# Three rings for FFN weight tiles, Down's raw weights issued five steps ahead, sums moved behind the lows, and first-visit banks copied by ScalarE

## The chip, the cores and the metric

The program runs on one core of one Trainium2 chip. The metric is the device time of one execution in microseconds (us). Engines: PE is TensorE (matmuls), DVE is VectorE, ACT is ScalarE, POOL is GpSimd, SP is SyncE (it only issues DMAs here).

## The reference

One inference step of a decoder layer for 512 prompt rows and 32 sample rows (544 columns in the kernel): stick-breaking attention and gated DeltaNet on one projection, cross attention, then SwiGLU. The change is in the last part, where D_MODEL is 2048 and FFN_HIDDEN is 5632, all in fp32:

```python
x = x + concat([o_sb, o_gdn]) @ p['w_out']
...
x = x + xo @ p['w_xo']
hf = rmsnorm(x, p['norm_ffn_g'])
gate, up = jnp.split(hf @ p['w_gate_up'], 2, axis=-1)
x = x + (jax.nn.silu(gate) * up) @ p['w_down']
```

## The kernel before

**Numbers.** An fp32 product is made of three matmuls in a reduced type (fp32r): hi·hi, hi·lo, lo·hi. For a weight tile, ScalarE casts the high part (`wh`) and VectorE subtracts it from the tile, which gives the low part (`wl`). Both FFN products use a scheme of 7 block products in place of 8 (products q = 1 to 7), so that four of the products take sums and differences of weight blocks; VectorE makes these (`sum`).

**Order.** `Work` is a table written out by hand: `at(tick, place, do)`. Ticks run upward, within a tick the places run upward, and each engine gets its instructions in that order. No engine waits for a tick: an engine goes on with the next instruction as soon as what it needs is there. So the table sets what is queued behind what on each engine.

**Gate/up** (class `GateUp`, 44 columns j, 7 ticks each): `load` issues four raw weight blocks of 512 KB on SP ("21", "11", "22", "12"), `sum` makes four differences (L1711), `high` (L1718) and `low` (L1722) split each of the seven left operands, `matmuls` (L1729) does 24 matmuls of 128x272 per tick. The hidden activations `u` are cast to `hs` and stored to DRAM (`hT`, by SP), to be fetched later by POOL's queue as `pr` operands of Down.

**Down** begins at tick `t_down` = 308 and has 88 steps (class `Step`) of 42 matmuls (L1783), one step a tick, for pairs of output columns m and groups g of hidden rows. A step loads its raw weights with two DMAs of 256 KB (L1750, tile `raw`), makes three sums (`sums`, L1760 to L1762), two highs (`high`, L1767: 0 of the raw weights, 1 of the sums) and two lows (`low`, L1773). It accumulates in four PSUM banks, P16 (128x544), P7 (128x272), P45 and P23 (128x544). Step p's loads stand at tick p − 4, its sums at p − 2, its highs and lows at p − 1.

A block of output columns is visited several times, and between visits the banks are kept in SBUF (tiles `a`). `take` does that: on the first visit VectorE copies P16 and P7 (L1833) and ScalarE P45 and P23 (L1831); on a middle visit VectorE adds P16 and P7 to what was kept (L1835), while P45 and P23 are read back and seeded: ScalarE's `before` (L1811) copies the kept part into the bank ahead of the next visit of that block. On the last visit `combine` joins the banks (ScalarE's s1, L1843; VectorE's L1844, L1846, L1848, L1849, L1851), and `out` transposes the results on TensorE into one PSUM tile (`aux`, L967), scales them on ScalarE (`y`, L2046) and stores them. The three parts of `out` stand at places 32.5 and 35.5 of the next tick and 32.5 of the one after. Steps 0 to 7 are the first visits of the eight blocks (group 0), 8 to 11 are group 1 of one half, 12 to 19 take groups 1 and 2 by turns, 20 to 71 the groups up to 8 in the same way, and 72 to 87 are the last visits, two steps each (groups 9 and 10). On first and last visits the products stand in the order 1, 6, 7, 4, 5, 2, 3, on middle visits 4, 5, 2, 3, 1, 6, 7, so that there P16's bank is touched only after 24 of the 42 matmuls.

**Tiles.** All weight tiles have one size (128x1024 fp32). `Ffn.tile` takes `wl` and raw "12" from a ring of 4 (`vp`) and everything else (raw, sums, `wh`) from one ring of 9 (`wp`). A tile of a ring waits for the last reader of the one that had the slot before. `fetch` (L1954) gets the `pr` operands of a group, 14 tiles of 272 KB, spread over ticks.

Of the kernel before, what the change touches and what calls it, by code (L numbers as in the profile page):

```python
# [8 lines left out]
F32 = mybir.dt.float32  # L9
F32R = mybir.dt.float32r  # L10
# [5 lines left out]
P = 128  # L16
# [24 lines left out]
W_TILES = 13  # L41
# [1606 lines left out]
class GateUp:  # L1648
# [3 lines left out]
    def __init__(self, f, j):  # L1652
# [5 lines left out]
        for x, tick in (("21", -8), ("11", -8), ("22", -7), ("12", -3)):  # L1658
            at(self.t0 + tick, 5, lambda x=x: self.load(x))
# [41 lines left out]
    def load(self, x):  # L1701
        f, c0 = self.f, self.cols[x[0] == "2"]
        self.a[x] = f.tile(F32, "raw", x == "12")
# [3 lines left out]
    def sum(self, q):  # L1707

        x, y = {5: ("21", "22"), 7: ("21", "11"), 6: ("22", 7), 3: ("12", 6)}[q]
        self.a[q] = self.f.tile(F32, "sum")  # L1710
# [5 lines left out]
    def high(self, q):  # L1716
        self.hi[q] = self.f.tile(F32R, "wh")
        self.f.c.nc.scalar.copy(self.hi[q], self.left(q))  # L1718

    def low(self, q):  # L1720
        self.lo[q] = self.f.tile(F32R, "wl", True)
# [17 lines left out]
class Step:  # L1739
# [5 lines left out]
    def load(self):  # L1745
        raw = self.f.tile(F32, "raw")
# [9 lines left out]
    def sums(self):  # L1756

        a, v = self.raw, self.c.nc.vector
        self.sum = b = self.f.tile(F32, "sum").rearrange("p (s m) -> p s m", s=4)
# [4 lines left out]
    def high(self, i):  # L1764
        x = (self.raw[:, 1:], self.sum)[i]
        hi = self.f.tile(F32R, "wh").rearrange("p (s m) -> p s m", s=4)[:, : 3 + i]
# [3 lines left out]
    def low(self, i):  # L1770
        x = (self.raw[:, 1:], self.sum)[i]
        lo = self.f.tile(F32R, "wl", True).rearrange("p (s m) -> p s m", s=4)[:, : 3 + i]
# [16 lines left out]
class Down:  # L1789
# [35 lines left out]
    def take(self, bank):  # L1825
# [4 lines left out]
        elif bank in (P45, P23):  # L1830
            self.c.nc.scalar.copy(x, self.c.bank[bank])  # L1831
        elif new:
            self.c.nc.vector.tensor_copy(x, self.c.bank[bank])  # L1833
# [20 lines left out]
class Ffn:  # L1854
# [29 lines left out]
    def tile(self, dt, name, own=False):  # L1884

        return (self.c.vp if own else self.c.wp).tile([P, 8 * P], dt, tag="w", name=name, bufs=4 if own else W_TILES - 4)

# [73 lines left out]
    def down(self):  # L1961
# [11 lines left out]
        tiles = [(pair, n, k) for n in (3, 1, 2, 0) for pair in range(2) for k in range(2 if n else 1)]  # L1973
        for g in range(11):
            a, b = used[g - 3][1] + 1 if g > 2 else (0, 0, 5)[g], used[g][0] - 1
            for i, x in enumerate(tiles):
                tick = t0 + a + i * (b - a) // 14 if g else t0 - (6 if i < 6 else 4)
# [4 lines left out]
    def step(self, p, s, nb):  # L1982

        at, tick, b = self.work.at, self.t_down + p, s.block
        seed = lambda block, *banks: [block.before(x) for x in banks if block]

        early = lambda n: tick - n if p >= n else self.t_down - 2 * (n - p)
        at(early(4) if p >= 4 else self.t_down - 12 + 2 * p, 95, s.load)

        place = lambda n, x, y: (early(n), x if early(n) >= self.t_down else y)  # L1990
        at(*place(2, 25, 62), s.sums)
        for i in range(2):
            at(early(1), 20 + i, lambda i=i: s.high(i))
# [243 lines left out]
```

## Time and profile before

| | us |
|---|---|
| median of 3 runs (lowest to highest) | 2971.8 (2969.07 to 2971.97) |
| the profiled execution | 2973.26 |
| its span in the profile | 2971.3 |
| mean granted clock of TensorE | 0.991 of full speed |

Gate/up runs from about 1530 to 2457 of the span, Down from 2457 to 2964. The profile shows when each engine worked, what each instruction waited for, and the chain of work that ended last. Idle time counts where TensorE is held up, since it is the engine with the most work.

### The profile page before, as it was taken

How to read it: one execution, taken by the hardware profiler on the slowest of the kernel's cores; microseconds unless marked ns; L12 is line 12 of the kernel's file. 1: busy time of each engine (PE TensorE's matmuls, PEld its weight loads, DVE VectorE, ACT ScalarE, POOL GpSimd, SP SyncE). 2: the span in 40 equal slices, each digit the busy share in tenths (PEclk: the TensorE clock that was granted, in tenths of full speed). 3: DMA queues.
4: the chain of work that ended last, by engine and by line, in shares of the span. 5: the costliest groups of instructions: out<-in, count | busy, mean ns of one | idle time of the engine just before them, and what ended most of it. 6: DMA issues, size and time to landing. Idle time of an engine off the chain costs nothing.

```text
span 2971.3 us, 56668 instructions
## 1 busy us (share of the span) xinstructions
PE 2868.1 (97%) x22122; PEld 2769.5 (93%) x22122; DVE 2079.2 (70%) x3334; ACT 1485.9 (50%) x2812; POOL 673.1 (23%) x916
## 2 busy tenths in 40 slices
PE   8999999999999999999979999999999999999999
PEld 7999999889899989998769999999999998999999
DVE  5776775655656665446488788878787777777786
ACT  5545443444555564334564444444444445445666
POOL 3211212312112100003222333333323234110110
PEclk9999999999999999999989999999999999999999
DMA  7323233454553684533444555555554558666653
GB/s 218 91 76 91 78 88 94 131 156 125 156 151 108 187 262 143 151 98 90 161 123 134 163 169 163 157 156 165 165 153 149 159 174 249 199 200 181 197 161 110
DMA packets 640420, 444.37 MB, mean 150 GB/s; under 512 B 36411, under 2 KB 566664, under 8 KB 640152
## 3 DMA queue, kind: packets, MB, share of 16 engines
q1 hardware_dynamic: 608328, 386.31, 44.3%
q0 software_dynamic: 22176, 42.90, 4.7%
q10 hardware_dynamic: 9648, 11.54, 1.1%
q8 instruction: 174, 2.85, 0.4%
q14 instruction: 94, 0.77, 0.1%
HBM read 360.07 MB, written 80.58 MB: 148 GB/s over the span
## 4 chain that ended last, share of the span: by engine, by line
PE 55%; DMA 4%; DVE 3%; ACT 1%; issue 1%; SPq 0%; ACTq 0%; DVEq 0%
PE gu L1729 31%; PE bank L1783 11%; PE mm L215 7%; DMA raw<-in_w_down 3%; PE aux L1349 2%; PE mm L1537 2%; DVE wl L1773 1%; PE aux L967 1%; PE aux L757 0%; DMA wr<-in_w_xo 0%; DVE sum L1760 0%; DVE sum L1761 0%; PE aux L706 0%; DVE wl L204 0%; DMA mem<-in_mem_prompt 0%
## 5 line engine op out<-in xcount | busy, mean ns | idle before, releaser
L1729 PE MATMUL gu<-pr,wh 128*128 128x272 f32 x4928 | 673.0, 289 | 6.8 <-ACT pr L1604 5.6
L1729 PEld LDWEIGHTS gu<-pr,wh 128*128 128x128 f32 x4928 | 640.4, 189 | 9.3 <-ACT pr L1604 6.8
L215 PE MATMUL mm<-ah,wh 128*128 128x272 f32 (+1 forms) x2464 | 537.6, 298 | 5.1 <-ACT ah L328 4.0
L215 PE MATMUL mm<-al,wh 128*128 128x272 f32 (+1 forms) x2464 | 523.4, 291 | 0.7 <-DVE al L246 0.7
L215 PE MATMUL mm<-ah,wl 128*128 128x272 f32 (+1 forms) x2464 | 514.9, 289 | 0.1
L1783 PE MATMUL bank<-pr,wh 128*128 128x272 f32 x2464 | 473.4, 291 | 8.5 <-DVE a L1833 4.5
L215 PEld LDWEIGHTS mm<-ah,wh 128*128 128x128 f32 (+1 forms) x2464 | 391.1, 188 | 28.3 <-issue 8.5
L1783 PEld LDWEIGHTS bank<-pr,wh 128*128 128x128 f32 x2464 | 391.2, 191 | 10.5 <-ACT bank L1811 4.8
L204 DVE TENSOR_TENSOR wl<-wr,wh 128x512 fp32r<-128x512 f32 (+1 forms) x366 | 262.0, 720 | 193.9 <-ACT wh L203 183.9
L215 PEld LDWEIGHTS mm<-al,wh 128*128 128x128 f32 (+1 forms) x2464 | 388.6, 188 | 5.4 <-issue 2.0
L203 ACT CAST wh<-wr 128x512 fp32r<-128x512 f32 (+1 forms) x366 | 224.4, 616 | 332.1 <-PE mm L215 272.4
L215 PEld LDWEIGHTS mm<-ah,wl 128*128 128x128 f32 (+1 forms) x2464 | 385.6, 188 | 2.5 <-DVE wl L204 0.5
L1783 PE MATMUL bank<-pr,wl 128*128 128x272 f32 x1232 | 359.2, 292 | 13.6 <-DVE wl L1773 12.6
L1729 PE MATMUL gu<-pr,wl 128*128 128x272 f32 x2464 | 359.7, 288 | 1.3 <-DVE wl L1722 1.3
L1729 PEld LDWEIGHTS gu<-pr,wl 128*128 128x128 f32 x2464 | 328.3, 189 | 1.6 <-DVE wl L1722 1.6
L1718 ACT CAST wh<-sum 128x1024 fp32r<-128x1024 f32 x176 | 185.0, 1051 | 175.5 <-DVE wl L1722 162.6
L1722 DVE TENSOR_TENSOR wl<-sum,wh 128x1024 fp32r<-128x1024 f32 x176 | 228.6, 1299 | 33.9 <-ACT wh L1718 30.3
L1783 PEld LDWEIGHTS bank<-pr,wl 128*128 128x128 f32 x1232 | 235.2, 191 | 17.7 <-DVE wl L1773 17.7
L1718 ACT CAST wh<-raw 128x1024 fp32r<-128x1024 f32 x132 | 139.0, 1053 | 107.6 <-DVE sum L1711 83.9
L1722 DVE TENSOR_TENSOR wl<-raw,wh 128x1024 fp32r<-128x1024 f32 x132 | 189.5, 1435 | 0.1
L1711 DVE TENSOR_TENSOR sum<-raw,sum 128x1024 f32<-128x1024 f32 x88 | 115.8, 1316 | 99.8 <-PE gu L1729 99.8
L1954 POOL DMA_DIRECT2D pr<-hT x154 | 81.8, 548 | 272.9 <-PE bank L1783 247.9
(530 smaller groups left out, 4331.4 us busy)
## 6 DMA issues: line engine op xcount, KB each, us to landing
raw<-in_w_gate_up SPq DMA_DIRECT2D x176, 512.0 KB
wr<-in_w_in SPq DMA_DIRECT2D x108, 512.0 KB
raw<-in_w_down SPq DMA_DIRECT2D x176, 256.0 KB
hT<-hs SPq DMA_DIRECT2D x154, 272.0 KB
pr<-hT POOLq DMA_DIRECT2D x154, 272.0 KB, 6.6
page<-in_cache_sb_k SPq DMA_DIRECT2D x128, 128.0 KB
page<-in_cache_sb_v SPq DMA_DIRECT2D x64, 256.0 KB
wr<-in_w_out SPq DMA_DIRECT2D x32, 512.0 KB
```

Source lines behind the costliest of these rows:

```text
L203: nc.scalar.copy(hi[:, :m, :n], raw[:, k : k + m, :n])
L204: nc.vector.tensor_sub(lo[:, :m, :n], raw[:, k : k + m, :n], hi[:, :m, :n].bitcast(F32))
L215: c.nc.tensor.matmul(ps[:n, h, :HT], l[:, :n], r[:, h * HT : (h + 1) * HT], start=first and i == 0, stop=last and i == 2,)
L967: c.nc.tensor.transpose(ps[:, a * P : (a + 1) * P], src[:, a * P : (a + 1) * P], c.ident)
L1349: nc.tensor.matmul(ps[:, :256], l, r, start=k == 0 and n == 0, stop=k == 7 and n == 2)
L1537: nc.tensor.matmul(ps[:, 0, :HT], l, r[:, cols], start=k == 0 and i == 0, stop=k == 3 and i == 2)
L1711: self.f.c.nc.vector.tensor_sub(self.a[q], self.a[x], self.a[y])
L1718: self.f.c.nc.scalar.copy(self.hi[q], self.left(q))
L1722: self.f.c.nc.vector.tensor_sub(self.lo[q], self.left(q), self.hi[q].bitcast(F32))
L1729: self.f.c.nc.tensor.matmul(bank, w[:, i * P : (i + 1) * P], self.f.pairs[i].op[q][r], start=q in (1, 5) and n == 0, stop=n == 23, skip_gr ...
L1783: self.c.nc.tensor.matmul(self.c.bank[bank][:, o], t[x][:, s, i * P : (i + 1) * P], pairs[i].op[q][r], start=new and not (i or n), stop=se ...
L1954: self.c.nc.gpsimd.dma_start(t, self.hT[2 * g + pair, :, max(0, 2 * n - 1) + k])
```

## The change

Tiles come from three rings: `vp` of 4 for `wl` and raw "12" as before; `wa` of 4 for all `wh` and gate/up's sums 5 and 3; `wp` of 5 for gate/up's raws "21", "11", "22" and sums 7 and 6, and for Down's raws and sums by turns. So in Down raw p takes the slot of the sum of step p − 4, and the sum of step p the slot of raw p − 1. Gate/up's raw "22" is loaded at tick −5 in place of −7.

Down's raws are loaded at tick p − 5 (steps 0 and 1 at −8, step 2 at −5, 3 at −4, 4 at −1). The sums of step k + 2 stand at place 52 of tick k, behind the lows of k + 1 (places 31 and 50) and ahead of the takes (60, 61), where they stood at 25, ahead of both lows. First visits copy all four banks on ScalarE, in the order P16, P7, P45, P23. Group 2's fetches start at tick 7 after `t_down` (they started at 5), group 3's at 13 (8); the others as before. Lines below the first lie 1 lower in the new file (L1760 becomes L1759), and from `take` on 3 lower.

```diff
...
-W_TILES = 13
...
@@ -1655,7 +1654,7 @@
         self.cols = k * P, HID + k * P
         self.a, self.hi, self.lo = {}, {}, {}
         at = f.work.at
-        for x, tick in (("21", -8), ("11", -8), ("22", -7), ("12", -3)):
+        for x, tick in (("21", -8), ("11", -8), ("22", -5), ("12", -3)):
             at(self.t0 + tick, 5, lambda x=x: self.load(x))
         for q, tick in ((7, -4), (5, -3), (6, -2), (3, 1)):
             at(self.t0 + tick, 50, lambda q=q: self.sum(q))
@@ -1700,25 +1699,25 @@
 
     def load(self, x):
         f, c0 = self.f, self.cols[x[0] == "2"]
-        self.a[x] = f.tile(F32, "raw", x == "12")
+        self.a[x] = f.tile(F32, "raw", f.c.vp) if x == "12" else f.tile(F32, "raw", f.c.wp, 5)
         w = f.c.w_gu.rearrange("(i t p) m -> t p i m", t=2, p=P)[x[1] == "2"]
         f.c.nc.sync.dma_start(self.a[x].rearrange("p (i m) -> p i m", m=P), w[:, :, c0 : c0 + P])
 
     def sum(self, q):
 
         x, y = {5: ("21", "22"), 7: ("21", "11"), 6: ("22", 7), 3: ("12", 6)}[q]
-        self.a[q] = self.f.tile(F32, "sum")
+        self.a[q] = self.f.tile(F32, "sum", self.f.c.wp, 5) if q in (7, 6) else self.f.tile(F32, "sum", self.f.c.wa)
         self.f.c.nc.vector.tensor_sub(self.a[q], self.a[x], self.a[y])
 
     def left(self, q):
         return self.a[{1: "11", 2: "12", 4: "22"}.get(q, q)]
 
     def high(self, q):
-        self.hi[q] = self.f.tile(F32R, "wh")
+        self.hi[q] = self.f.tile(F32R, "wh", self.f.c.wa)
         self.f.c.nc.scalar.copy(self.hi[q], self.left(q))
 
     def low(self, q):
-        self.lo[q] = self.f.tile(F32R, "wl", True)
+        self.lo[q] = self.f.tile(F32R, "wl", self.f.c.vp)
         self.f.c.nc.vector.tensor_sub(self.lo[q], self.left(q), self.hi[q].bitcast(F32))
 
     def matmuls(self, q):
@@ -1743,7 +1742,7 @@
         self.f, self.c, self.block, self.visit, self.g, self.first, self.last = f, f.c, block, visit, g, first, last
 
     def load(self):
-        raw = self.f.tile(F32, "raw")
+        raw = self.f.tile(F32, "raw", self.c.wp, 5)
         self.raw = raw.rearrange("p (s t i m) -> p s t (i m)", s=2, t=2, i=2)
 
         for s, m in ((1, self.block.m), (0, self.block.m + 1)):
@@ -1756,20 +1755,20 @@
     def sums(self):
 
         a, v = self.raw, self.c.nc.vector
-        self.sum = b = self.f.tile(F32, "sum").rearrange("p (s m) -> p s m", s=4)
+        self.sum = b = self.f.tile(F32, "sum", self.c.wp, 5).rearrange("p (s m) -> p s m", s=4)
         v.tensor_sub(b.rearrange("p (x s) m -> p x s m", s=2)[:, :, 0], bc(a[:, 0:1], [P, 2, 2 * P]), a[:, 1:3])
         v.tensor_sub(b[:, 1], a[:, 1], b[:, 2])
         v.tensor_sub(b[:, 3], a[:, 3], b[:, 1])
 
     def high(self, i):
         x = (self.raw[:, 1:], self.sum)[i]
-        hi = self.f.tile(F32R, "wh").rearrange("p (s m) -> p s m", s=4)[:, : 3 + i]
+        hi = self.f.tile(F32R, "wh", self.c.wa).rearrange("p (s m) -> p s m", s=4)[:, : 3 + i]
         self.c.nc.scalar.copy(hi, x)
         self.hi = (self.hi + [hi]) if i else [hi]
 
     def low(self, i):
         x = (self.raw[:, 1:], self.sum)[i]
-        lo = self.f.tile(F32R, "wl", True).rearrange("p (s m) -> p s m", s=4)[:, : 3 + i]
+        lo = self.f.tile(F32R, "wl", self.c.vp).rearrange("p (s m) -> p s m", s=4)[:, : 3 + i]
         self.c.nc.vector.tensor_sub(lo, x, self.hi[i].bitcast(F32))
         self.lo = (self.lo + [lo]) if i else [lo]
 
@@ -1827,10 +1826,8 @@
         new, x = bank not in self.parts, self.part(bank)
         if self.x and self.x[0] == bank:
             self.c.nc.vector.tensor_add(x, halves(self.x[1]), self.c.bank[bank])
-        elif bank in (P45, P23):
+        elif new or bank in (P45, P23):
             self.c.nc.scalar.copy(x, self.c.bank[bank])
-        elif new:
-            self.c.nc.vector.tensor_copy(x, self.c.bank[bank])
         else:
             self.c.nc.vector.tensor_add(x, x, self.c.bank[bank])
 
@@ -1881,9 +1878,9 @@
         self.t_down = 7 * NH
         self.down()
 
-    def tile(self, dt, name, own=False):
-
-        return (self.c.vp if own else self.c.wp).tile([P, 8 * P], dt, tag="w", name=name, bufs=4 if own else W_TILES - 4)
+    def tile(self, dt, name, pool, bufs=4):
+
+        return pool.tile([P, 8 * P], dt, tag="w", name=name, bufs=bufs)
 
     def open(self):
 
@@ -1971,9 +1968,11 @@
                 used.setdefault(g, [len(steps), 0])[1] = len(steps)
                 steps.append(Step(self, downs[m], count[m], g, g == groups[0], g == groups[-1]))
         tiles = [(pair, n, k) for n in (3, 1, 2, 0) for pair in range(2) for k in range(2 if n else 1)]
+
+        begin = [0, 0, used[1][0] - 1, used[2][0]]
         for g in range(11):
-            a, b = used[g - 3][1] + 1 if g > 2 else (0, 0, 5)[g], used[g][0] - 1
             for i, x in enumerate(tiles):
+                a, b = begin[g] if g < 4 else used[g - 3][1] + 1, used[g][0] - 1
                 tick = t0 + a + i * (b - a) // 14 if g else t0 - (6 if i < 6 else 4)
                 at(tick, 90, lambda g=g, i=i, x=x: self.fetch(g, i, *x))
         for p, s in enumerate(steps):
@@ -1983,15 +1982,17 @@
 
         at, tick, b = self.work.at, self.t_down + p, s.block
         seed = lambda block, *banks: [block.before(x) for x in banks if block]
-
-        early = lambda n: tick - n if p >= n else self.t_down - 2 * (n - p)
-        at(early(4) if p >= 4 else self.t_down - 12 + 2 * p, 95, s.load)
-
-        place = lambda n, x, y: (early(n), x if early(n) >= self.t_down else y)
-        at(*place(2, 25, 62), s.sums)
+        if p > 1:
+            at(tick - 5 if p > 4 else self.t_down - (5, 4, 1)[p - 2], 95, s.load)
+            sums, highs, lows = (tick - 2, 52), (tick - 1, 20), (tick - 1, 31)
+        else:
+
+            at(self.t_down - 8, 95, s.load)
+            sums, highs, lows = (((tick - 3, 62), (tick - 2, 20), (tick - 2, 62)), ((tick - 2, 65), (tick - 1, 20), (tick - 1, 31)))[p]
+        at(*sums, s.sums)
         for i in range(2):
-            at(early(1), 20 + i, lambda i=i: s.high(i))
-            at(*place(1, (31, 50)[i], 63 + i), lambda i=i: s.low(i))
+            at(highs[0], highs[1] + i, lambda i=i: s.high(i))
+            at(lows[0], lows[1] + (0, 19)[i], lambda i=i: s.low(i))
         if p == 0:
             at(tick, 28, lambda: (self.c.open_banks(), b.next_visit()))
         for i in range(7):
@@ -2008,10 +2009,12 @@
             at(tick, 34, lambda: seed(nb, P16, P7))
             at(tick, 60, lambda: (b.combine(1), seed(nb, P45)))
             at(tick, 61, lambda: (b.combine(2), seed(nb, P23), self.out(tick, b, nb is None)))
+        elif s.visit:
+            at(tick, 60 if s.first else 32.5, lambda: (b.take(P45), seed(nb, P45)))
+            at(tick, 60, lambda: (b.take(P23), seed(nb, P23)))
+            at(tick, 61, lambda: (b.take(P16), b.take(P7), seed(nb, P16, P7)))
         else:
-            at(tick, 60 if s.first else 32.5, lambda: (b.take(P45), seed(nb, P45)))
-            at(tick, 60, lambda: s.visit and (b.take(P23), seed(nb, P23)))
-            at(tick, 61, lambda: (b.take(P16), b.take(P7), s.visit or (b.take(P23), seed(nb, P23)), seed(nb, P16, P7)))
+            at(tick, 60, lambda: [(b.take(x), seed(nb, x)) for x in (P16, P7, P45, P23)])
 
     def out(self, tick, b, last):
 
@@ -2187,7 +2190,7 @@
     phase.close()
 
 
-    c.hp, c.vp, c.wp = (ctx.enter_context(tc.tile_pool(name=x, bufs=3)) for x in ("hp", "vp", "wp"))
+    c.hp, c.vp, c.wa, c.wp = (ctx.enter_context(tc.tile_pool(name=x, bufs=3)) for x in ("hp", "vp", "wa", "wp"))
 
     aux = ctx.enter_context(tc.tile_pool(name="auxf", bufs=1, space=PSUM))
     c.aux = lambda: aux.tile([P, 512], F32, tag="aux", name="aux", bufs=1)
```

VectorE at the end of one last visit and in the next, before. `raw`, `wh`, `sum` and `wl` are weight tiles, `a` with numbers are kept parts, `bank` with numbers the PSUM banks; the first row is the second low of the step, the three after it are the combines:

```order
L1773 TENSOR_TENSOR wl<-sum,wh 128x1024
L1848 TENSOR_TENSOR a_29998<-a_30002,bank_29505 128x272
L1849 TENSOR_TENSOR a_29996<-a_30002,bank_29505 128x544
L1851 TENSOR_TENSOR a_30002<-a_29998,bank_29506 128x544
L1760 TENSOR_TENSOR sum<-raw 128x2x256
L1761 TENSOR_TENSOR sum<-raw,sum 128x256
L1762 TENSOR_TENSOR sum<-raw,sum 128x256
L1773 TENSOR_TENSOR wl<-raw,wh 128x768
L1773 TENSOR_TENSOR wl<-sum,wh 128x1024
```

The same place after the change:

```order
L1772 TENSOR_TENSOR wl<-sum,wh 128x1024
L1759 TENSOR_TENSOR sum<-raw 128x2x256
L1760 TENSOR_TENSOR sum<-raw,sum 128x256
L1761 TENSOR_TENSOR sum<-raw,sum 128x256
L1845 TENSOR_TENSOR a_29998<-a_30004,bank_29507 128x272
L1846 TENSOR_TENSOR a_30002<-a_30004,bank_29507 128x544
L1848 TENSOR_TENSOR a_30004<-a_29998,bank_29508 128x544
L1772 TENSOR_TENSOR wl<-raw,wh 128x768
L1772 TENSOR_TENSOR wl<-sum,wh 128x1024
```

The three sums, which stood right behind the last combine, now stand between the second low and the first combine. TensorE's order is the same in both kernels.

ScalarE at the start of Down, before, from the highs of step 1 on (step 0's copies follow them; of the banks, numbered in this order, 29503 is P16, then P7, P45 and P23, and after the change 29505 to 29508):

```order
L1767 CAST wh<-raw 128x768
L1767 CAST wh<-sum 128x1024
L1831 COPY a_29553<-bank_29505 128x544
L1831 COPY a_29559<-bank_29506 128x544
L1767 CAST wh<-raw 128x768
```

And after:

```order
L1766 CAST wh<-raw 128x768
L1766 CAST wh<-sum 128x1024
L1830 COPY a_29559<-bank_29505 128x544
L1830 COPY a_29561<-bank_29506 128x272
L1830 COPY a_29563<-bank_29507 128x544
L1830 COPY a_29565<-bank_29508 128x544
L1766 CAST wh<-raw 128x768
```

Each first visit has two copies more, of P16 (128x544) and of P7 (128x272), ahead of those of P45 and P23; VectorE has two copies fewer.

SyncE at the start of Down, before (`hT<-hs` stores the hidden activations, `raw` with two DMAs a step):

```order
L1750 DMA raw<-in_w_down 128x4x128 x2
L1945 DMA hT<-hs 128x544 x2
L1705 DMA raw<-in_w_gate_up 128x8x128
L1750 DMA raw<-in_w_down 128x4x128 x2
L1945 DMA hT<-hs 128x544 x2
L1750 DMA raw<-in_w_down 128x4x128 x2
L1945 DMA hT<-hs 128x544 x2
L1750 DMA raw<-in_w_down 128x4x128 x6
L1945 DMA hT<-hs 128x544
L1750 DMA raw<-in_w_down 128x4x128 x2
```

And after:

```order
L1942 DMA hT<-hs 128x544 x2
L1749 DMA raw<-in_w_down 128x4x128 x4
L1942 DMA hT<-hs 128x544 x2
L1749 DMA raw<-in_w_down 128x4x128 x10
L1942 DMA hT<-hs 128x544
L1749 DMA raw<-in_w_down 128x4x128 x2
L1942 DMA hT<-hs 128x544 x2
L1749 DMA raw<-in_w_down 128x4x128 x4
```

The raws of steps 0 and 1 now go out together, and those of steps 2 to 6 in one run, ahead of the store that stood behind step 5's raw; from there on every store stands behind one raw more.

## Rows read from the trace of the kernel before

**Rows 1.** The page's part 1: busy time, share of the span and instructions of each engine.

```profile
PE 2868.1 (97%) x22122; PEld 2769.5 (93%) x22122; DVE 2079.2 (70%) x3334; ACT 1485.9 (50%) x2812; POOL 673.1 (23%) x916
```

**Rows 2.** Stretches of the span with TensorE alone: from and to, length, busy time and (x) instructions, granted clock as a share of 2.4 GHz, busy share of the DMA engines, GB/s.

```profile
1600.00:2457.00 857.00, 856.95 (x6843) 1.00 0.54 161
2457.00:2500.00 43.00, 38.52 (x283) 0.92 0.60 172
2500.00:2540.00 40.00, 34.63 (x259) 1.00 1.07 313
2540.00:2720.00 180.00, 172.89 (x1343) 0.98 0.65 194
2720.00:2870.00 150.00, 145.58 (x1143) 0.99 0.64 186
2870.00:2964.00 94.00, 93.28 (x755) 1.00 0.40 115
```

**Rows 3.** The chain of work that ended last, in order of time: start, length, engine or DMA, output tile, line, and how many instructions stand in the step.

```profile
1600.49 856.89 PE gu L1729 x6840
...
2505.18 13.58 DMA raw<-in_w_down
...
2521.81 11.43 DMA raw<-in_w_down
...
2621.98 11.99 DMA raw<-in_w_down
...
2828.55 11.99 DMA raw<-in_w_down
...
2888.00 3.01 PE bank L1783 x24
...
2899.62 3.01 PE bank L1783 x24
```

**Rows 4.** What TensorE waited for from 2440 to the end: waiting engine, tile and line, what released it, us in total, times, longest.

```profile
PE bank L1783 <- DVE wl L1773: 12.6, 9, 2.2
PE bank L1783 <- DVE a L1833: 4.5, 3, 3.4
PE bank L1783 <- ACT bank L1811: 4.0, 4, 2.2
```

**Rows 5.** TensorE in order of time at the start of Down: start, length, engine, line, operation, output and inputs, and in brackets the idle time before it and what ended it.

```profile
2466.16 0.79 PE L1783 MATMUL bank<-pr,wh 128*128 128x272 f32 x2 [3.36 <-DVE a L1833]
2466.75 0.43 PE L1783 MATMUL bank<-pr,wl 128*128 128x272 f32 x1
...
2471.74 0.47 PE L1783 MATMUL bank<-pr,wh 128*128 128x272 f32 x2
...
2472.17 0.41 PE L1783 MATMUL bank<-pr,wh 128*128 128x272 f32 x2
```

**Rows 6.** A stretch of 20 us, columns as in rows 2.

```profile
2460.00:2480.00 20.00, 16.64 (x113) 0.83 0.34 94
```

**Rows 7.** VectorE in order of time at the start of Down, columns as in rows 5.

```profile
2460.29 0.69 DVE L1760 TENSOR_TENSOR sum<-raw 128x512 f32<-128x512 f32 x1
...
2462.73 1.52 DVE L1773 TENSOR_TENSOR wl<-raw,wh 128x768 fp32r<-128x768 f32 x1
...
2465.31 1.06 DVE L1833 COPY a<-bank 128x544 f32<-128x544 f32 x2
```

**Rows 8.** VectorE eight to nine steps later.

```profile
2505.79 1.06 DVE L1833 COPY a<-bank 128x544 f32<-128x544 f32 x2
2511.77 0.69 DVE L1760 TENSOR_TENSOR sum<-raw 128x512 f32<-128x512 f32 x1 [4.92 <-DMA raw<-in_w_down]
```

**Rows 9.** DMA queues from 2498 to 2533: packets, MB, share of 16 engines' time. The software queue carries `pr`, the hardware queue mostly `raw`.

```profile
q0 software_dynamic: 4596, 8.89, 78.5%
q1 hardware_dynamic: 5444, 3.12, 37.4%
```

**Rows 10.** ScalarE at the start of Down, columns as in rows 5.

```profile
2472.74 0.61 ACT L1831 COPY a<-bank 128x544 f32<-128x544 f32 x1 [7.57 <-PE bank L1783]
```

**Rows 11.** VectorE at the change from the middle visits to the last visits, and in one last visit.

```profile
2870.41 1.18 DVE L1835 TENSOR_TENSOR a<-a,bank 128x544 f32<-128x544 f32 x2 [0.53 <-PE bank L1783]
...
2882.87 0.72 DVE L1851 TENSOR_TENSOR a<-a,bank 128x544 f32<-128x544 f32 x1
2883.51 0.68 DVE L1760 TENSOR_TENSOR sum<-raw 128x512 f32<-128x512 f32 x1
...
2885.04 0.96 DVE L1773 TENSOR_TENSOR wl<-raw,wh 128x768 fp32r<-128x768 f32 x1
...
2888.67 0.69 DVE L1760 TENSOR_TENSOR sum<-raw 128x512 f32<-128x512 f32 x1 [1.46 <-PE bank L1783]
...
2893.20 0.43 DVE L1848 TENSOR_TENSOR a<-a,bank 128x272 f32<-128x272 f32 x1
...
2894.36 0.72 DVE L1851 TENSOR_TENSOR a<-a,bank 128x544 f32<-128x544 f32 x1
```

**Rows 12.** ScalarE in the same last visit.

```profile
2885.86 1.13 ACT L2046 ACTIVATE y<-aux,unscale 128x128 f32<-128x128 f32 x4
2888.04 1.14 ACT L2046 ACTIVATE y<-aux,unscale 128x128 f32<-128x128 f32 x4 [1.05 <-PE aux L967]
```

**Rows 13.** TensorE in the same last visit: the second set of transposes.

```profile
2887.40 0.60 PE L967 MATMUL aux<-ident,a 128*128 128x128 f32 x4
```

**Rows 14.** What VectorE waited for in gate/up, columns as in rows 4.

```profile
DVE sum L1711 <- PE gu L1729: 97.6, 40, 3.0
```

**Rows 15.** VectorE in gate/up: from and to, length, busy time and (x) instructions, granted clock, DMA share, GB/s.

```profile
1600.00:2440.00 840.00, 678.73 (x681) 1.00 0.53 158
```

**Rows 16.** The page's part 6: DMA issues, KB each, median us from issue to landing.

```profile
pr<-hT POOLq DMA_DIRECT2D x154, 272.0 KB, 6.6
```

## The prediction, made before the changed kernel was run

> **What bounds the kernel now.** Four views, in this order. The page's first part says which engine to follow: TensorE is busy for 97% of the span, VectorE for 70%, ScalarE for 50% [rows 1]. So time is saved only where TensorE idles or runs slowly, and the reader should look for those places. The chain of waits gives the price of work without gaps: 6840 gate/up matmuls in 856.89 us, 125.3 ns each [rows 3]. With that price the table of stretches tells where time is lost, as length minus instructions times 125.3 ns [rows 2]. Gate/up: 857.0 − 6843 × 0.1253 = 0, nothing. Down: 2457 to 2500, 43 − 283 × 0.1253 = 7.5 us; 2500 to 2540, 7.5; 2540 to 2720, 11.7; 2720 to 2870, 6.8; the last visits after 2870, none. The sum is 33.5 us, and no edit to Down's first 72 steps can bring more.
>
> What the losses are is read from the waits of TensorE: 12.6 us for VectorE's `wl`, 4.5 for its bank copies (L1833), 4.0 for ScalarE's bank seeds [rows 4]. These are 21.1 us; the other 12 us are slow matmuls behind the waits. The first wait of 3.36 us shows this: from 2466.16 to 2471.74 two hi matmuls and one lo take 0.68 us where they take 0.37 later, and the stretch's granted clock is 0.83 [rows 5, 6]. Those are the chip's levels of 1.2 and 2.4 GHz; the 24 matmuls took 5.58 us in place of 3.0.
>
> Two causes lie behind the waits. At 2465.31 VectorE copies step 0's banks only after sums and both lows (2460.29 to 2465.3, two of them stretched) [rows 7], while ScalarE is idle for 7.57 us until 2472.74 [rows 10]. And in the chain, each later `wl` goes back to a `raw` DMA of 11.4 to 13.6 us ([rows 3] has four of them); VectorE sits 4.92 us at the head of its queue, in the sums of two steps ahead, with the lows of the next step behind it [rows 8].
>
> **What goes.** *Opening, −7.5 us (2457 to 2500).* P16 and P7 move to ScalarE: a VectorE copy pair of 1.06 us goes from each of 8 steps, and a ScalarE copy of 0.61 (128x544) and one of some 0.4 (half as wide) come in, 8.1 us in all, into an engine that waited 7.57 us at this very point [rows 7, 10]. Sums now stand behind the lows of the next step, so the lows no longer wait for them. If ScalarE's gap were not there, the cost would be the 1.0 us per step.
>
> *Raw waits, −26 us (2500 to 2870).* A raw load took the slot which the low of step p−3 freed; now it takes the one of the sum of p−4, about one step of 5.26 us earlier, less 1 us because the second low frees it and not the first. Also, a late raw now holds up only the sums and the kept parts (takes) behind them, no longer the next lows. The next visit of a bank needs the take only 24 matmuls into a step (3.01 us, [rows 3]). That is some 2.5 to 3.5 us later. Together a raw may be about 7 to 8 us later than before. In the later bursts one step loses about 4 us each, which fits with room. In the first burst the lag adds up over four steps to 7.5 us, which just fits; besides, group 3's fetches begin 5 ticks later, out of that burst. I leave 1.0 us there (bounds 0 and 7.5).
>
> *Gate/up rings, 0.* VectorE waited 97.6 us for TensorE before sums there [rows 14], because one ring tied the sum to an unrelated tile; the ring by kind loosens that. TensorE did not wait, so nothing is gained. Raw "22" issues two ticks later. It still leads its sum (place 5 of tick −5 to place 50 of −3) by some 2.9 ticks × 3.01 us = 8.7 us, above the 6.6 us that the `pr` transfers take [rows 16]. The start of gate/up changes order slightly: 0, bounds ±1.5.
>
> **What comes.** *Opening, +2.0 us (0.3 to 5).* Raws 0 and 1 are issued together, raw 2 at tick −5 and raw 3 at −4, both amid group 0's `pr` fetch; before, only raw 3 was. 0.52 MB more at 350 GB/s or so (8.89 + 3.12 MB in 35 us, [rows 9]) is 1.5 us by which the last `pr` tiles of step 0 are late. And VectorE now has sums 1 (1.6 to 2.4 us) ahead of gate/up's last products and of the lows of step 1: 0.5.
>
> *Step 7 to 8, +0.5 (0 to 1).* P45's copy and seed wait in ScalarE behind P16 and P7 copies of 1.0 us. *Step 71 to 72, +1.0 (0 to 3).* The take at 2870.41 starts 0.53 us after the lows [rows 11]; three sums of 1.53 us (2883.51 to 2885.04) now come first, and ScalarE's seed of the next block waits for it.
>
> *Last visits, +7.0 us (0 to 14).* This is the dearest part. Before, VectorE's order was last combine, sums, lows; now one set of sums stands between the low and the combines (order pieces above). Follow the loop of one block from combine (2882.87) to combine (2894.36). ScalarE: seed, two casts, the first `y` until 2886.99 (4.12 us). Then the second transposes at 2887.40, which share one PSUM tile with the first, and `y` at 2888.04 (0.64) [rows 11 to 13]. From there by casts, the s1 copy, additions and the low to 2893.20 (5.16), and to the last combine 1.16. That makes 11.1 us, against TensorE's block of 2899.62 − 2888.00 = 11.62 us [rows 3]: hidden, with `y` waiting 1.05 us for TensorE. With sums of 1.53 us inside, the loop is 12.6 us, longer than TensorE's, and TensorE waits at the second transposes because the first `y` still holds the tile: 1.0 us in each of seven blocks. At 14 us each such wait would cost double, by slow matmuls; the waits seen with a slow clock behind them were longer (2.2 and 3.4 us).
>
> **Sum.** −33.5 + 1.0 + 2.0 + 0.5 + 1.0 + 7.0 = −22.0 us. The profiled execution took 2973.3 us, which gives 2951.3; the median of the runs shown is 1.5 us lower, so I forecast 2949.7, rounded to 2949.5.
>
> **The rivals.** *1. The last visits stay hidden.* Then 7.0 us do not come, and if the opening is also clean the time is 2971.8 − 33.5 + 2.5 = 2941. For it: VectorE is idle for 1.46 us ahead of the sums at 2888.67 [rows 11], time that a set of sums would fit in. Against it: the idle time doesn't lie between the low and the combine, where the sums now stand.
>
> *2. Issuing earlier does not get raw weights sooner.* In the burst the two queues moved 4596 and 5444 packets, nearly alike, and raw got 3.12 MB of 12.0 [rows 9], 5.9 raws in 35 us where steps of 5.26 us use 6.7. If that share holds, a longer lead only puts off the lag; if the lead were used up in each burst, the 26 us stay, only the opening's 7.5 goes, and 10.5 come: 2971.8 + 3.0 = 2975, no change that can be told. Against it: the lag in one burst is 0.8 raws, 4 us, less than the added lead, and between bursts it is made up (DMA busy 0.64 in 2720 to 2870, [rows 2]). The Trainium skill, "DMA: Bandwidth & Descriptors", section "Queues, rings and completion order", says that an engine takes turns between queue rows packet by packet; the like counts of packets agree. By that rule alone the share of raw would not grow with depth, which is this rival.
>
> *3. Slower: gate/up comes to wait for raw "22".* The place is the sum 5 of each of 44 periods; ring and tick leave it about 8.7 us of lead. VectorE is busy for 678.73 of 840 us there, 81% [rows 15], so a late sum is not made up within the period. If the load, behind `hT` stores on SyncE's queue, lands after 9.7 us, TensorE loses 1.0 us × 44 = 44 us: 2949.5 + 44 = 2993.5. It decides from 0.5 us of lateness (+22 us, the whole gain). For it: raws in Down took 11 to 13 us [rows 3]. Against it: those were bursts, and in gate/up the DMA engines are busy for 0.54 of the time [rows 2].
>
> *4. The waits of 1 us in the last visits pull the clock down* as the 3.36 us did (2.6 us each): 7 × 2.6 = 18 more, 2967.5.
>
> **How the numbers follow.** Forecast 0.55 (its own range 2941 to 2958), rival 1 0.17, rival 2 0.12, rival 3 0.07, rival 4 0.05, and 0.04 for a lesser gain with several terms at their bad ends. About 0.2%, 6 us, is what a measurement of this kernel can tell from no change. Faster by more: forecast, rival 1, half of rival 4 and of the rest, with some room for errors in the terms: 0.80. Within it: rival 2 and the rest, 0.13. Slower: rival 3 with 0.07. The range from 2936 to 2969 takes in forecast, rival 1 and rival 4; rivals 2 and 3 are left out.
>
> **What would show it.** Right: no wait of 3 us at 2463 and granted clock 1.00 around 2470; in 2500 to 2870 losses, by length minus count times 125.3 ns, below 2 us; `DMA raw<-in_w_down` gone from the chain; in the last visits a new wait of TensorE in the transposes (L967 or its new line) on ScalarE's `y`, about 1 us, seven times. Wrong: DVE sums that wait for `raw` for over 5 us with TensorE idle behind them (rival 2); a TensorE wait in gate/up (rival 3); last visits at 11.62 us per block (rival 1).

## The result and the profile after

The changed kernel took 2953.09 us (median of 6 runs, 2949.16 to 2956.47), the kernel before beside it 2970.95 (2968.77 to 2971.97): a ratio of 0.9941 with an interval of 0.9928 to 0.9953, 17.9 us less. The profiled execution took 2949.16 us with a span of 2947.4, the quickest of the six.

Part of the spread has nothing to do with Down. In the profiles of the changed kernel and of the six below that are built on it, the code ahead of Down is the same, yet Down's first matmul comes anywhere from 2453.76 to 2461.21. So beside the medians this text gives the length of Down: the span less the start of Down's first matmul. It is of one execution each, so how much it varies is not known. Before it is 2971.3 − 2457.22 = 514.1 us, after 2947.4 − 2455.92 = 491.5: 22.6 us less.

The page's part 1, busy time by engine, answers to [rows 1]. TensorE is as busy as before, in a shorter span:

```profile
PE 2857.2 (97%) x22122; PEld 2762.0 (94%) x22122; DVE 2102.3 (71%) x3318; ACT 1494.0 (51%) x2828; POOL 728.3 (25%) x916
```

The stretches of TensorE alone, columns as in [rows 2], are read in the same way (length minus instructions times 125.3 ns):

```profile
2457.00:2500.00 43.00, 43.00 (x345) 1.00 0.81 232
2500.00:2540.00 40.00, 37.80 (x292) 0.96 1.00 296
2540.00:2720.00 180.00, 179.19 (x1429) 1.00 0.72 209
2720.00:2850.00 130.00, 129.28 (x1036) 1.00 0.65 188
```

Losses: −0.2 (nothing), 3.4, 0.9 and 0.2 us, where the kernel before lost 7.5, 7.5, 11.7 and (to 2870) 6.8. What TensorE still waits for, from 2440 on, answers to [rows 4]:

```profile
PE aux L966 <- ACT y L2049: 6.2, 7, 0.9
PE bank L1782 <- ACT bank L1810: 3.7, 3, 2.2
```

Of the waits before, those for `wl` (12.6 us) and for VectorE's bank copies (4.5) are gone. A wait in the transposes is new. So is most of the wait for ScalarE's seeds: of its three, only the 0.72 us at 2840 stands in the same place as before (0.72 us at 2871 there). The other two are 2.20 us at 2532 and 0.81 us at 2576. The next rows show the cause of the first, in the burst near 2500 to 2540.

SyncE's queue, with twelve raw DMAs in one run and then `xl` (the block's part of the residual x, that P45 or P23 takes once):

```profile
2492.56 31.08 SPq L1749 DMA_DIRECT2D raw<-in_w_down  x12
2523.69 2.05 SPq L1806 DMA_DIRECT2D xl<-xq  x1
```

VectorE, ScalarE and TensorE behind it:

```profile
2530.64 0.72 DVE L1828 TENSOR_TENSOR a<-xl,bank 128x544 f32<-128x544 f32 x1 [2.43 <-DMA xl<-xq]
2531.28 1.22 DVE L1772 TENSOR_TENSOR wl<-sum,wh 128x1024 fp32r<-128x1024 f32 x1
```

```profile
2531.40 0.62 ACT L1810 COPY bank<-a 128x544 f32<-128x544 f32 x1 [2.91 <-DVE a L1828]
```

```profile
2532.07 0.82 PE L1782 MATMUL bank<-pr,wh 128*128 128x272 f32 x2 [2.20 <-ACT bank L1810]
```

Read from the top: `xl` is issued only at 2523.69, as the raws ahead of it wait for their slots; VectorE's take of P45 (L1828) waits 2.43 us for it, at the head of the queue; ScalarE's seed of the next visit waits 2.91 us for the take; TensorE waits 2.20 us for the seed. Two hi matmuls take 0.82 us behind it, against 0.41 at full clock, so here too a slow stretch follows. At 2576 the same comes back: VectorE waits 4.41 us for `xl`, and TensorE 0.81. So in this burst TensorE's delay goes back to `xl`, where before it went back to `raw`.

A last visit, in the order of [rows 11 to 13]: VectorE from the second low (L1772) over the sums to the first combine (L1845), then ScalarE's two `y` behind that combine (L2049, which was L2046), then TensorE's second transposes, of the block before and between these two `y`:

```profile
2874.37 1.22 DVE L1772 TENSOR_TENSOR wl<-sum,wh 128x1024 fp32r<-128x1024 f32 x1
2875.51 0.68 DVE L1759 TENSOR_TENSOR sum<-raw 128x512 f32<-128x512 f32 x1
...
2877.03 0.43 DVE L1845 TENSOR_TENSOR a<-a,bank 128x272 f32<-128x272 f32 x1
```

```profile
2881.18 1.13 ACT L2049 ACTIVATE y<-aux,unscale 128x128 f32<-128x128 f32 x4
2883.11 1.14 ACT L2049 ACTIVATE y<-aux,unscale 128x128 f32<-128x128 f32 x4 [0.80 <-ACT y L2049]
```

```profile
2869.60 0.66 PE L966 MATMUL aux<-ident,a 128*128 128x128 f32 x4 [0.88 <-ACT y L2049]
...
2882.37 0.66 PE L966 MATMUL aux<-ident,a 128*128 128x128 f32 x4 [0.93 <-ACT y L2049]
```

The sums take 2875.51 to 2877.03 between low and combine; the second transposes wait 0.88 and 0.93 us for the first `y`; and a block takes 2882.37 − 2869.60 = 12.77 us where it took 11.62.

Gate/up: from 1600 on TensorE waits nowhere (857.00 us busy of 857). VectorE's waits there, columns as in [rows 4], show that the 97.6 us of [rows 14] are gone, while the waits for ScalarE's casts have grown from 26.2 to 87.1 us; one raw was 0.9 us late for a sum:

```profile
DVE wl L1721 <- ACT wh L1717: 87.1, 98, 1.8
...
DVE sum L1710 <- DMA raw<-in_w_gate_up: 0.9, 1, 0.9
```

### The profile page after: what moved, and what is told of

It reads as the page before. It is cut to its first block, busy times and chain, and to the rows that moved or that the text cites. A ratio compares the mean times of both kernels' runs of the same rounds, so it can differ in the third digit from the quotient of the medians.

```text
span 2947.4 us, 56985 instructions
## 1 busy us (share of the span) xinstructions
PE 2857.2 (97%) x22122; PEld 2762.0 (94%) x22122; DVE 2102.3 (71%) x3318; ACT 1494.0 (51%) x2828; POOL 728.3 (25%) x916
## 5 line engine op out<-in xcount | busy, mean ns | idle before, releaser
L1782 PE MATMUL bank<-pr,wh 128*128 128x272 f32 x2464 | 466.9, 289 | 3.7 <-ACT bank L1810 3.7
L1721 DVE TENSOR_TENSOR wl<-sum,wh 128x1024 fp32r<-128x1024 f32 x176 | 219.0, 1244 | 81.4 <-ACT wh L1717 81.4
L1721 DVE TENSOR_TENSOR wl<-raw,wh 128x1024 fp32r<-128x1024 f32 x132 | 206.9, 1567 | 15.9 <-ACT wh L1717 14.0
L1710 DVE TENSOR_TENSOR sum<-raw,sum 128x1024 f32<-128x1024 f32 x88 | 142.7, 1622 | 0.6
```

The lines of the kernel that those rows point to most:

```text
L1710: self.f.c.nc.vector.tensor_sub(self.a[q], self.a[x], self.a[y])
L1721: self.f.c.nc.vector.tensor_sub(self.lo[q], self.left(q), self.hi[q].bitcast(F32))
L1782: self.c.nc.tensor.matmul(self.c.bank[bank][:, o], t[x][:, s, i * P : (i + 1) * P], pairs[i].op[q][r], start=new and not (i or n), stop=se ...
```

## Experiments

Medians are of 4 to 11 runs, which lie within 2 to 7 us of each other, so that 3 us between two variants are little more than the noise. Each ratio is to the kernel before as it ran beside that variant (medians of 2970.0 to 2971.4). "Down" is the length defined above, of the one profiled execution.

| kernel | median us | against before (interval) | Down us |
|---|---|---|---|
| before | 2970.95 | | 514.1 |
| changed | 2953.09 | 0.9941 (0.9928 to 0.9953) | 491.5 |
| last sums behind combines | 2942.95 | 0.9905 (0.9889 to 0.9920) | 486.1 |
| xl early, residual left out | 2947.09 | 0.9921 (0.9907 to 0.9934) | 486.6 |
| xl early | 2946.69 | 0.9909 (0.9894 to 0.9924) | 486.3 |
| both mends | 2938.48 | 0.9884 (0.9869 to 0.9900) | 480.8 |
| both mends, copies on VectorE | 2941.53 | 0.9897 (0.9881 to 0.9912) | 484.3 |
| changed, copies on VectorE | 2952.15 | 0.9940 (0.9926 to 0.9953) | 493.9 |
| before, sums behind the lows | 2959.52 | 0.9965 (0.9952 to 0.9979) | 499.9 |
| before, copies on ScalarE | 2967.58 | 0.9985 (0.9976 to 0.9994) | 510.5 |
| before, all order, no rings | 2941.83 | 0.9906 (0.9889 to 0.9922) | 483.4 |

### The sums of the last visits put back

```diff
-            sums, highs, lows = (tick - 2, 52), (tick - 1, 20), (tick - 1, 31)
+            sums, highs, lows = (tick - 2, 62 if p > 72 else 52), (tick - 1, 20), (tick - 1, 31)
```

> The changed kernel, but the sums of steps 73 on stand behind the combines and takes (place 62) as before, not between the low and the combine. Theory (the sums lengthen the loop combine, y, transposes, casts, low, combine past TensorE's 11.62 us per block): the seven waits of TensorE in the transposes on ScalarE's y (6.2 us in the changed kernel) go, a block of the last visits takes 11.6 us again in place of 12.77, and the time falls by 7 to 9 us, to about 2945. Rival (the second y is late for another reason, such as ScalarE's longer queue or the earlier raws): the waits stay, blocks keep 12.7 us, time within 2 us of the changed kernel's 2953.

Measured: 2942.95 us, 10.1 less than the changed kernel. The waits in the transposes are gone. Of TensorE's waits from 2440 on the only sizeable one left is that for the seeds, and the stretch 2870 to 2930 has no gap (60 us busy of 60; the changed kernel had 56.29). First the wait, then the stretch:

```profile
PE bank L1782 <- ACT bank L1810: 5.6, 3, 3.8
```

```profile
2870.00:2930.00 60.00, 60.00 (x488) 1.00 0.38 110
```

The theory holds, and its price was a little low: seven blocks of 1.15 us are 8.0 us. Down became only 5.4 us shorter, since in this profile the wait for `xl` is longer (3.79 us in place of 2.20) and 2500 to 2540 loses 40 − 272 × 0.1253 = 5.9 us in place of 3.4; with these 2.5 us it is 7.9. The medians' 10.1 us is 2 us more than the rows account for.

```profile
2500.00:2540.00 40.00, 36.21 (x272) 0.91 0.99 292
```

### The residual loaded two ticks earlier

```diff
-            at(tick, 29.6, lambda x=b.fresh.pop(0): b.load(x))
+            at(tick - 2, 29.6, lambda x=b.fresh.pop(0): b.load(x))
```

> The changed kernel, but the residual tiles xl are loaded two ticks earlier, so that on SyncE they stand ahead of two raw loads that they stood behind. Theory (the waits left at 2532 and 2576 come from xl, issued behind raws that wait for room in the burst; VectorE's take of P45 stands before the next low and ScalarE's seed behind it): VectorE's 8.1 us of waits on xl fall below 2, TensorE's 2.2 and 1.0 us waits for the bank seeds there go, with the slow clock behind the first; 3 to 5 us less than the changed kernel. Rival (the burst is bound by bytes, so that something else in it is late): the wait moves to a raw or a pr tile of the same steps, and the time stays within 2 us.

This edit did more than its words say: `next_visit` clears the block's note of `xl` after the early load, so that P45 and P23 were kept by a plain ScalarE copy and the residual was left out. Its 2947.09 us only bounds what the waits for `xl` are worth, with the add gone as well. The edit that keeps the add puts `xl` to use at its old tick:

```diff
+    def use(self):
+        self.x = self.next
...
+            at(tick - 2, 29.6, lambda x=b.fresh.pop(0): b.load(x))
+            at(tick, 29.6, b.use)
```

> The changed kernel with xl loaded two ticks earlier and put to use at its old tick, so that the residual is added as before. Theory (xl stands behind raws on SyncE, and VectorE's take and ScalarE's seed behind xl): no wait of VectorE for xl above 1 us, TensorE's waits for bank seeds fall from 3.7 to about 0.7 us, no loss in 2500 to 2540 (3.4 us in the changed kernel); 2946 to 2949. Rival (the burst's bytes are late whichever stands first): a raw or pr is late by the same 2 to 4 us and the time stays at 2951 to 2955.

Measured: 2946.69 us, 6.4 less than the changed kernel. The stretch 2500 to 2540 has no loss left (322 × 0.1253 = 40.3), at a DMA share of 1.14, so the burst's bytes did not bind; the seeds' waits fell from 3.7 to 0.7 us. The theory holds. The stretch, and TensorE's waits from 2440 on:

```profile
2500.00:2540.00 40.00, 40.00 (x322) 1.00 1.14 335
```

```profile
PE aux L966 <- ACT y L2054: 6.2, 7, 1.0
PE bank L1782 <- ACT bank L1814: 0.7, 1, 0.7
```

### Both mends

The two edits together.

> The changed kernel with both: sums of steps 73 on behind combines and takes, and xl loaded two ticks earlier. If the two losses are separate, their gains add: 10 us from the first (2942.95 alone) and 4 to 6 from the second, so 2936 to 2939; if the shorter time of one is taken up by the other, about 2942.

Measured: 2938.48 us, the quickest of all, 14.6 us below the changed kernel where the two alone give 10.1 and 6.4. The gains nearly add, and by Down they add in full: 10.7 us, from 5.4 and 5.2. In its profile a little is left in the burst, with a take behind sums that waited for a raw (TensorE's waits from 2440 on):

```profile
PE bank L1782 <- ACT bank L1814: 1.4, 2, 0.7
PE bank L1782 <- DVE a L1836: 0.9, 1, 0.9
```

### Copies of the first visits back on VectorE

```diff
-        elif new or bank in (P45, P23):
+        elif bank in (P45, P23):
             self.c.nc.scalar.copy(x, self.c.bank[bank])
+        elif new:
+            self.c.nc.vector.tensor_copy(x, self.c.bank[bank])
```

> The changed kernel, but the first visits' P16 and P7 are copied by VectorE again. Theory of the prediction (the copies held up the opening, since VectorE had sums and lows ahead of them): of the 7.5 us that the stretch of the first eight steps lost before, 4 to 8 come back, with a wait of TensorE for VectorE's copy near 2463 and a slow clock behind it; about 2957 to 2961. Rival (the order of sums and the earlier raws cleared the opening, and VectorE has time for its copies): below 2 us come back, and VectorE's copies end before TensorE's next visit of the bank.

Measured: 2952.15 us against 2953.09, no difference that the medians can tell, though Down is 2.4 us longer in the profile (493.9 against 491.5). The opening is worse, as the theory has it: 43 − 299 × 0.1253 = 5.5 us lost to 2500, in waits for VectorE's copies of up to 1.4 us. The next stretch gives 3.0 us of it back: 0.4 us lost in 2500 to 2540 where the changed kernel lost 3.4. The stretches and TensorE's waits:

```profile
2457.00:2500.00 43.00, 38.77 (x299) 1.00 0.70 202
2500.00:2540.00 40.00, 39.59 (x316) 1.00 1.06 313
```

```profile
PE bank L1782 <- DVE a L1832: 4.1, 4, 1.4
PE bank L1782 <- ACT bank L1810: 1.9, 3, 0.7
```

So the theory was right about the opening and wrong about the time: the copies do hold TensorE up, but a TensorE that is later meets less of the wait for `xl`. The same undoing on top of both mends asks whether `xl` alone gave the time back:

> The version with both mends, and the first visits' copies on VectorE again. Theory (with VectorE's copies the opening loses 4.7 us in four waits, which was not seen in the time of the changed kernel only because a later start met less of the wait for xl): with xl mended the copies cost their 4 to 5 us in full, about 2941 to 2943. Rival (an opening that ends later is made up for anyway by the burst): within 1.5 us of the version with both mends.

Measured: 2941.53 us against 2938.48 (the intervals in the table overlap), and Down 484.3 against 480.8. The time is the theory's, its "in full" is not: the opening loses 43 − 302 × 0.1253 = 5.2 us, and the copies cost about 3. The 1.9 us that the version with both mends loses in 2500 to 2540 (40 − 304 × 0.1253) does not come here, so with `xl` out of the way, too, a later TensorE meets less of what is late in the burst. The opening here, the burst with both mends alone, and here what TensorE waited for VectorE:

```profile
2457.00:2500.00 43.00, 38.94 (x302) 1.00 0.75 215
```

```profile
2500.00:2540.00 40.00, 38.40 (x304) 1.00 1.04 310
```

```profile
PE bank L1782 <- DVE a L1836: 3.9, 4, 1.4
```

### One part alone in the kernel before: ScalarE's copies

The edit to `take` the other way round, with the order P16, P7, P45, P23.

> The kernel before with one part of the change: first visits' banks copied by ScalarE. Theory (the opening's waits for VectorE's copies are real, but in the kernel before whatever the opening gains only brings TensorE sooner to raws that are late): the wait of 3.36 us goes, the stretch to 2500 loses 2 to 4 us in place of 7.5, and the time falls by less than that, 0 to 4 us. Rival (each stretch's loss stands for itself, as the prediction had it): the full 5 us or more, near 2965.

Measured: 2967.58 us, 3.8 less. Losses by stretch are 2.0, 10.4, 10.8 and 7.3 us: 5.5 us less to 2500 than before, 2.9 us more in the next 40. The stretches:

```profile
2457.00:2500.00 43.00, 41.58 (x327) 1.00 0.70 202
2500.00:2540.00 40.00, 34.36 (x236) 0.91 0.99 293
2540.00:2720.00 180.00, 173.46 (x1350) 0.98 0.67 198
2720.00:2850.00 130.00, 125.67 (x979) 0.99 0.67 193
```

The theory holds, the time falling short of the opening's gain: TensorE came sooner to raws that are late. The interval of the ratio (1.8 to 7.1 us) does not exclude the rival's 5 us by itself; the burst's 2.9 us more speak against it.

### One part alone in the kernel before: sums behind the lows

```diff
-        at(*place(2, 25, 62), s.sums)
+        at(*place(2, 52, 62), s.sums)
```

> The kernel before with one part of the change: the sums of step k+2 at place 52 (behind the lows of k+1), in the old ring of 9 and with raws at p-4. Theory (the raw waits went by two things, the lead of one step and the order that lets a late raw hold up the takes and no longer the lows): a part of the 26 us of 2500 to 2870 goes, 5 to 15, the opening keeps its wait for VectorE's bank copies, and the last visits lose the same 7 us; about 2963 to 2973. Rival 1 (the order alone took the raw waits): 2500 to 2870 loses under 4 us and the time is near 2955. Rival 2 (the lead alone did): 2500 to 2870 still loses 24 us or more and the time is about 2978.

Measured: 2959.52 us, with the waits in the transposes (6.3 us, so some 8 us of the last visits are in it). In 2540 to 2850 nothing is lost; in 2500 to 2540 4.2 us are, in waits for takes (L1835); the opening's waits for VectorE's copies (L1833) stay, and it loses 8.8 us in place of 7.5. Stretches and waits:

```profile
2457.00:2500.00 43.00, 36.67 (x273) 0.96 0.59 166
2500.00:2540.00 40.00, 36.37 (x286) 1.00 1.11 327
2540.00:2720.00 180.00, 180.00 (x1438) 1.00 0.73 213
2720.00:2850.00 130.00, 130.00 (x1042) 1.00 0.66 192
```

```profile
PE bank L1783 <- DVE a L1833: 6.3, 4, 3.5
PE aux L967 <- ACT y L2046: 6.3, 7, 1.0
PE bank L1783 <- DVE a L1835: 3.6, 2, 2.3
```

One line in the old ring, with raws at p − 4, takes all of the raw waits but those of the first burst: some 22 of the 26 us, where the theory had 5 to 15. That is nearly rival 1 in the stretches, though not in the time, as the opening and the last visits stay dear.

### All of the order, none of the rings

The kernel before with the last two edits, and the sums of steps 73 on at place 62.

> The kernel before with its one ring of 9 and raws at p-4, plus every change of order: sums behind the lows (those of steps 73 on behind combines and takes, as in the mended version) and first-visit banks copied by ScalarE. Not in it: the three rings, the lead of five steps, gate/up's raw 22, the later fetches. Theory (the order took the raw waits, and the rings with the fifth step of lead bring next to nothing that can be seen): 2459.52 is the sums alone at 2959.52, less 7 us for the last visits, less about 4 for the copies, so 2946 to 2950 if the two waits that the first burst left there (1.4 and 2.5 us) stay or grow, and 2940 or less if they go. Rival (the lead is worth its 4 to 8 us once the opening is quicker, since the burst is reached sooner): 2948 to 2955, with waits of TensorE for VectorE's takes of 4 us or more and a slow clock behind them in 2500 to 2540.

Measured: 2941.83 us. Only the first burst still loses, 4.3 us in three waits of at most 1.6 us for takes (L1833 in this file) behind a late raw; stretches and waits:

```profile
2457.00:2500.00 43.00, 43.00 (x343) 1.00 0.77 218
2500.00:2540.00 40.00, 36.08 (x285) 1.00 1.02 302
2540.00:2720.00 180.00, 180.00 (x1438) 1.00 0.72 211
2720.00:2850.00 130.00, 129.28 (x1035) 1.00 0.66 191
```

```profile
PE bank L1783 <- DVE a L1833: 3.9, 3, 1.6
PE bank L1783 <- ACT bank L1811: 0.7, 1, 0.7
```

The time lies between the theory's two values: waits in the first burst stayed, and for that case it had 2946 to 2950. It put the copies at 4 us, but with the sums behind the lows the opening lost 8.8 us without them and loses nothing here.

Against the version with both mends (2938.48; Down 483.4 against 480.8) the rings, the fifth step of lead and the later fetches together are worth about 3 us, which is not clear of the noise, as the two intervals in the table overlap. Which of the three brings it was not tried. In the changed kernel as it is they also brought the waits for `xl`, worth 6.4 (5.2 by Down). The rings and the lead with the old order of sums were not tried: with five slots the sum of step k + 2 needs the slot of raw k + 1, whose low would stand behind it on VectorE.

## Why the prediction was right or wrong

**The time.** Forecast 2949.5, measured 2953.09, in the range of 2936 to 2969 and on the side forecast. The sum said −22.0 us; Down became 22.6 us shorter in the profiled execution, and the medians differ by 17.9. That the sum comes so near is in part luck, since its errors cancel: costs of 3.5 us did not come (opening 2.0, steps 7 to 8 and 71 to 72 1.5), while 2500 to 2850 lost 3.5 us more than the 1.0 put down, and the last visits cost 1.0 us more. What the sum left out is the burst's wait for `xl`, which ran to 2.20 us in the changed kernel's profile and to 3.79 us in that with the last sums put back. How long it is in the executions without a profile is not known, so it is open how much of the 4.7 us between the two differences, 22.6 and 17.9, is its.

**The opening, −7.5 + 2.0.** The loss to 2500 went entirely, and the +2.0 did not come: no gap is left in that stretch. By the experiments 5.5 us of it belong to the copies on ScalarE, and the rest to the order of sums and lows together with them; the order without the copies left 8.8 us. What failed is the assumption that a stretch's gain reaches the end: alone in the kernel before, the 5.5 us gave 3.8, and in the changed kernel undoing them made Down 2.4 us longer, since the next burst took up the other 3.0.

**The raw waits, −26 + 1.0.** They went, but the earlier slot was not needed for most of them. The order alone, in the old ring, cleared 2540 to 2850; on top of it the lead, with the rings and the later fetches, matters in the first burst only, for about 3 us. No run has the lead without the order, so the 4 to 5 us of slack that the prediction put on the earlier slot are neither shown nor refuted. The step that failed in this term is the 1.0 us left over: it was mis-sized and mis-placed. 4.5 us are left from 2500 to 2850, and the greater part waits for `xl`, not for a raw. The prediction counted what the moved loads do to `hT` stores and `pr` fetches and did not follow the third kind of DMA on SyncE's queue, which stands behind raws that now wait for a slot five steps ahead. Loading `xl` two ticks earlier took the waits away.

**Last visits, +7.0.** Right in place, count and cause: seven waits in the second transposes on the first `y`; 1.15 us per block where the loop gave 1.0. Putting the sums back gave it back. So the last visits were not hidden (rival 1). That each wait might pull the clock down (rival 4) did not happen: the seven waits are 0.9 us each, and the granted clock stayed at 1.00. The prediction's ground for that was too simple, though: it named only waits of 2.2 and 3.4 us as followed by a slow clock, but a wait of 1.95 us at 2843 in the kernel before was too (0.50 from 2844 to 2847).

**Steps 7 to 8 and 71 to 72, +1.5.** Neither came. At 71 to 72 TensorE waits 0.72 us as before: the raw is there early, so the sums are done before TensorE ends the step, and the take starts as soon as it did.

**Rivals.** Gate/up never waited for raw "22" (rival 3); one sum there waited 0.9 us for a raw, so some lead there was used up once between 1600 and 2440. Rival 2 (a burst that gives raw a fixed share) fell: with `xl` early nothing is lost in the burst at a DMA share of 1.14. Over 2498 to 2533 the two queues now moved these packets and MB, columns as in [rows 9]:

```profile
q0 software_dynamic: 3886, 7.50, 63.8%
q1 hardware_dynamic: 7002, 3.68, 44.5%
```

Raw's queue moved 7002 packets to 3886, no longer nearly alike, and 3.68 MB in place of 3.12. By the Trainium skill, "DMA: Bandwidth & Descriptors", section "Queues, rings and completion order", queues with work take turns packet by packet. These rows neither bear that out nor refute it, since group 3's fetches also start later and fewer `pr` transfers stand in the stretch; nor is it shown that what the profile counts as packets are the packets of that rule.

**The signs.** The opening's wait and its slow clock are gone, and the seven waits came, as said. The losses in 2500 to 2870 are not below 2 us. Whether `raw` left the chain cannot be read: in the changed kernel's profile the chain goes back only to 2931.

## What to carry to other kernels

Ask of a late transfer first what is queued behind the instruction that waits for it: moving that instruction behind work that is due sooner was one line, and took some 22 of 26 us of waits here; the deeper prefetch was worth about 3 us on top of it, and was not tried without it. When loads are issued further ahead, every other transfer on the same issuing queue now stands behind their waits for a slot, so those that are due soon (here the residual) are to be moved ahead of them. And an order that is right in one phase is to be checked in each phase: the same line cost 8 us in the last visits.

## What the runs showed of the hardware

The start of Down moved by 7.5 us (2453.76 to 2461.21) between executions with the same code ahead of it, more than several of the effects measured; that is why the length of Down stands beside the medians.

And TensorE's clock: behind the wait of 2.20 us matmuls ran at half speed (2532.07, granted clock 0.96 over 40 us), while stretches with waits of up to 1.65 us (the copies on VectorE, the order without the rings) show 1.00 throughout. The length of one wait alone did not decide it. Behind 1.67 us in the kernel before with ScalarE's copies the clock fell to 0.50, the level of 1.2 GHz; behind 2.33 us in the kernel before with the sums behind the lows it stayed at 1.00, to the end of its stretch 2540 to 2720 above. What else decides is open. First the shorter wait and the clock behind it, then the longer one:

```profile
2531.47 0.39 PE L1783 MATMUL bank<-pr,wl 128*128 128x272 f32 x1 [1.67 <-DVE wl L1773]
2534.00:2536.00 2.00, 2.00 (x11) 0.50 0.71 197
```

```profile
2537.47 0.52 PE L1783 MATMUL bank<-pr,wh 128*128 128x272 f32 x2 [2.33 <-DVE a L1835]
```
